# WKV recurrence on one core: loads moved to the SyncE queue, state rows to GpSimd, and a shorter state chain

## The chip, the core and the metric

The kernel runs on one core of a Trainium2 chip. The metric is the device time of one execution in microseconds (us). A core has a matrix engine (TensorE, PE in the profile), VectorE (DVE), ScalarE (ACT), GpSimd (POOL) and SyncE (SP). SP only issues transfers here; ACT and POOL can issue them too. All transfers are carried out by the core's 16 DMA engines. In the profile, transfers issued by POOL stand under the queue "software_dynamic", those issued by SP and ACT under "hardware_dynamic".

## The reference

For each of 16 batches and 256 channels the reference walks through 2048 time steps. Cut to what matters:

```
for t in range(seq_len):
    ww = u + k[t];  qq = max(pp, ww)
    e1, e2 = exp(pp - qq), exp(ww - qq)
    out[t] = (e1 * aa + e2 * v[t]) / (e1 * bb + e2 + 1e-08)
    ww = pp - w + k[t];  qq = max(ww, k[t])
    e1, e2 = exp(ww - qq), exp(k[t] - qq)
    aa, bb, pp = e1 * aa + e2 * v[t], e1 * bb + e2, qq
```

So the output is a weighted mean of all v so far, with weights exp(k) that decay by exp(-w) each step. `aa` and `bb` are numerator and denominator, `pp` is the running exponent that keeps them in range. Inputs k and v are 16 x 2048 x 256 float32 (33.5 MB each), and the output has the same size.

## The kernel before, in words

Time is cut into a head of 32 steps and 16 chunks ("steps" `c`, from 0 to 15) of 126 time steps. A chunk is worked on in four "pairs" `n` of four batches each; with two pairs for the head there are 66 pairs. A pair has time on the partitions and 4 batches x 256 channels along the free axis, so each of its three transfers (k in, v in, output) has about 512 KB.

The sum over time inside a chunk is a matrix product with triangular matrices. What comes from before the chunk, the state (the aa and bb above with their scale), is put into two extra rows (126 and 127) of the operand tiles `ez`. The state passes from chunk to chunk by a chain of small instructions on tiles of 128 partitions.

The main loop (L533) has one iteration per pair and works as a software pipeline. In iteration n:

- `load(n + 3)` starts the loads of `kr` and `vr`, each of which has four buffers (`AHEAD + 1`);
- ACT does `exps(n)` (L277), PE `sums(n - 1)` (L323), DVE rounds the next k, `round_k(n + 1)` (L258, tile `km`), and casts the next v, `cast_v(n + 1)` (L285, tile `vb`); DVE multiplies by v (L293);
- the output of a pair comes ten iterations after its exponentials (`LAG`): PE `den` and `num` (L457, L475), ACT the reciprocal as Ln and Exp (L465, L466), DVE `mult` (L483), and `store` (L499) for the pair of the iteration before.

Nothing is reordered by a planner: the helper `K` chains each instruction behind the last one of the same engine, so every engine and every issuing queue runs in the order in which Python emits it. That holds for the loads: those of pairs 0 to 3 are issued from SP (one of them from ACT), those of all later pairs from POOL (L121), where they stand in one line with the stores.

The state work of chunk c is spread by the table `later` (L503 to L516) over the iterations after the last pair of the chunk, s: the sums are copied and turned in s + 1 (`copy_sums`, `turn_sums`, `split_sums`). In s + 2 come the logs (`state_logs`, L352), the offsets S and exponents ex (`state_offsets`, L364 to L368), their exponentials g (`state_weights`, L375), and then the chain itself (`state_chain`, L387 to L392), which advances the state by two half chunks: tile `AB` holds numerator and denominator at both half-chunk starts. In s + 3 come the weights under which the state is injected (`inject_min` L402 and L404, `inject_weights` L409), the product `carries` (L417), the turn on PE (L424), the copy to `row` (L429) and four small transfers of 8 KB from SP (L433) that write `row` into rows 126 and 127 of `ez`. The tiles `ez` with these rows are first needed by `den` in iteration s + 7.

Of the kernel before, what the change touches and what calls it, by code (L numbers as in the profile page):

```python
# [22 lines left out]
def kernel(  # L23
# [11 lines left out]
    def K(ins):  # L35

        block, e, new = nc.cur_bb.bb, ins.ins.engine, []
        for i in reversed(block.instructions):
            if i.engine == e:
                new.append(i)  # L40
                if i.name == pinned.get(e):
                    break
        for a, b in zip(new[1:], new):
            tc.add_manual_dep(b, a.name, mybir.DependencyInfo(
                mybir.DependencyClass.NoSync, mybir.DependencyReason.DATA), reason="order")
        pinned[e] = new[0].name
        return ins
# [5 lines left out]
    TC = 2 * HS  # L53
    T0 = T % TC
    NST = T // TC
# [6 lines left out]
    RS = 2.0 ** -43  # L62
    LNRS = 43 * 0.6931471805599453
    CAP = 68.0

    consts = ctx.enter_context(tc.tile_pool(name="consts", bufs=1))
    kpool = ctx.enter_context(tc.tile_pool(name="kpool", bufs=AHEAD + 1))
# [33 lines left out]
    def load(n):  # L101
        kr = kpool.tile([128, 4, Dm], F32, tag="kr", name="kr")
        vr = vpool.tile([128, 4, Dm], F32, tag="vr", name="vr")
        kr_of[n], vr_of[n] = kr, vr
        c, p = pairs[n]
        if is_head(n):
            if p == 1:
                K(POOL.memset(kr[64:96, 0:2, :], 0.0))
                K(POOL.memset(vr[64:96, 0:2, :], 0.0))
            for t, x in ((kr, k), (vr, v)):  # L110
                for g in range(NG):
                    b = 6 * g + 4 * p
                    e = min(b + 2 * tiles_of(n), B)
                    if b < e:
                        K(SP.dma_start(out=t[g * GB:(g + 1) * GB, 0:e - b, :],
                                        in_=x[b:e, 0:T0, :].rearrange("n t d -> t n d")))
        else:
            t0 = T0 + c * TC
            r = min(128, T - t0)
            for t, x, eng in ((kr, k, SP), (vr, v, SP if n else SC)):  # L120
                K((eng if n <= AHEAD else POOL).dma_start(  # L121
                    out=t[0:r, :, :], in_=x[4 * p:4 * p + 4, t0:t0 + r, :].rearrange("n t d -> t n d")))


# [34 lines left out]
    K(POOL.memset(I1, 0.0))  # L159
    select(I1, NE, 1.0, 0, -1, 128, 1)  # L160
    K(POOL.memset(cc[:, 4:5], 0.5))
    select(cc[:, 4:5], GE, 0.0, -HS, 1, 1, 0)
    select(cc[:, 4:5], GE, 0.0, TC - 1, -1, 1, 0)

# [139 lines left out]
    def group_of(c, j):  # L304
        return 2 * j if c == 0 else 1 + 2 * c + j
# [37 lines left out]
    def split_sums(c):  # L343
# [2 lines left out]
        K(DVE.tensor_copy(t.rearrange("p r (b k) -> p (r b) k", k=4), tt))  # L346
        st[c, "t"] = t

    def state_logs(c):
        lf = tiny.tile([128, 2, 32], F32, tag="lf", name="lf")  # L350
        H = 1 if c < 0 else 2
        K(SC.activation(lf[:, 0:H], st[c, "t"][:, 4:4 + H], ACT.Ln))  # L352
        st[c, "lf"] = lf

    def state_offsets(c):

        lf = st.pop((c, "lf"))
        S = small.tile([128, 3, 32], F32, tag="S", name="S")
        ex = tiny.tile([128, 4, 32], F32, tag="ex", name="ex")
        if c < 0:  # L360
            K(DVE.tensor_copy(S[:, 2, :], lf[:, 0, :]))
            K(DVE.scalar_tensor_tensor(ex[:, 2, :], S[:, 2, :], 0.0, lf[:, 0, :], ALU.max, ALU.subtract))
        else:
            K(DVE.tensor_copy(S[:, 0, :], st.pop((c - 1, "S"))[:, 2, :]))  # L364
            for h in range(2):
                K(DVE.scalar_tensor_tensor(S[:, h + 1, :], S[:, h, :], 0.0, lf[:, h, :], ALU.max, ALU.add))
            K(DVE.tensor_scalar(ex[:, 0:2, :], S[:, 1:3, :], -1.0, 0.0, ALU.mult, ALU.max))
            K(DVE.scalar_tensor_tensor(ex[:, 2:4, :], S[:, 1:3, :], 0.0, lf, ALU.max, ALU.subtract))  # L368
        st[c, "S"] = S
        st[c, "ex"] = ex  # L370

    def state_weights(c):
        g = tiny.tile([128, 4, 32], F32, tag="g", name="g")
        sl = slice(2, 3) if c < 0 else slice(0, 4)
        K(SC.activation(g[:, sl, :], st.pop((c, "ex"))[:, sl, :], ACT.Exp, scale=-2.0))  # L375
        st[c, "g"] = g

    def state_chain(c):

        g, t = st.pop((c, "g")), st.pop((c, "t"))[:, 0:4].rearrange("p (q h) x -> p q h x", q=2)  # L380
        nxt = small.tile([128, 2, 2, 32], F32, tag="AB", name="AB")
        if c < 0:
            K(DVE.tensor_mul(nxt[:, :, 0, :], t[:, :, 0, :], g[:, 2:3, :].broadcast_to([128, 2, 32])))
        else:
            cur = AB[c]
            tb = tiny.tile([128, 2, 2, 32], F32, tag="tb", name="tb")
            K(DVE.tensor_mul(tb, t, g[:, 2:4, :].unsqueeze(1).broadcast_to([128, 2, 2, 32])))  # L387
            for h in range(2):
                dst = cur[:, :, 1, :] if h == 0 else nxt[:, :, 0, :]
                da = tiny.tile([128, 2, 32], F32, tag=f"da{h}", name=f"da{h}")  # L390
                K(DVE.tensor_mul(da, cur[:, :, h, :], g[:, h:h + 1, :].broadcast_to([128, 2, 32])))
                K(DVE.tensor_add(dst, da, tb[:, :, h, :]))  # L392
        AB[c + 1] = nxt

    def inject_logs(c):
        y = tiny.tile([128, 2, 32], F32, tag="y", name="y")
        K(SC.activation(y, AB[c][:, 0], ACT.Ln, scale=RS))
        st[c, "y"] = y

    def inject_min(c):  # L400
        m = tiny.tile([128, 2, 32], F32, tag="m", name="m")
        K(DVE.tensor_scalar(m, st.pop((c, "y")), -0.5, 0.5 * (CAP - LNRS), ALU.mult, ALU.add))  # L402
        m2 = tiny.tile([128, 2, 32], F32, tag="m2", name="m2")
        K(DVE.scalar_tensor_tensor(m2, st[c, "S"][:, 0:2, :], 0.0, m, ALU.max, ALU.min))  # L404
        st[c, "m"] = m2

    def inject_weights(c):
        f = tiny.tile([128, 2, 32], F32, tag="phi", name="phi")
        K(SC.activation(f, st.pop((c, "m")), ACT.Exp, scale=2.0))  # L409
        st[c, "phi"] = f  # L410

    def carries(c):

        ab = tiny.tile([128, 2, 2, 2, 16], BF16, tag="ab16", name="ab16")
        cur, f = AB.pop(c), st.pop((c, "phi"))
        for h in range(2):
            K(DVE.tensor_mul(ab[:, h].rearrange("p j q x -> p q j x"),  # L417
                             cur[:, :, h, :].rearrange("p q (j x) -> p q j x", j=2),
                             f[:, h, :].rearrange("p (j x) -> p j x", j=2).unsqueeze(1).broadcast_to([128, 2, 2, 16])))
        st[c, "ab"] = ab  # L420

    def turn_carries(c):
        d = bank("den", [128, 2, D])[:, 0]
        K(PE.matmul(d[:, 0:128], st.pop((c, "ab")).rearrange("p h j q x -> p (h j q x)"), Id, start=True, stop=True))  # L424
        st[c, "d"] = d

    def inject(c):
        row = small.tile([128, 128], BF16, tag="row", name="row")
        K(DVE.tensor_copy(row, st.pop((c, "d"))[:, 0:128]))  # L429
        for j in range(2):  # L430
            for h in range(2):
                p = 64 * h + 32 * j
                K(SP.dma_start(out=EZ[group_of(c, j)][TC + h:TC + h + 1, 0:2, :, :].rearrange(  # L433
                                   "o q i (x c) -> o (q i x) c", c=128),
                               in_=row[p:p + 32, :]))

# [67 lines left out]
    for c in range(-1, NST):  # L504
        s = last_of[c]
        work = [(s + 1, "sums", copy_sums), (s + 1, "last", turn_sums)]
        if c < 0:
            work += [(s + 2, "sums", split_sums), (s + 2, "act", state_logs), (s + 2, "last", state_offsets),
                     (s + 3, "exp", state_weights), (s + 3, "pool", state_chain)]
# [93 lines left out]
```

## Time and profile before

| | |
|---|---|
| median of 13 runs | 366.59 us (364.08 to 371.74) |
| the profiled execution: its own time | 366.59 us |
| its span, first to last instruction | 364.9 us |
| busy in the span: PE, DVE, ACT, POOL | 291.1, 295.4, 279.4, 168.7 us |
| moved by the DMA engines | 102.59 MB, 281 GB/s over the span |
| of it on the queue that POOL feeds | 98.53 MB |
| mean of one load issue on POOL (kr, vr) | 797 ns, 774 ns |
| mean of one store issue on POOL | 1000 ns |
| median from issue to landing, loads of 512 KB from POOL (kr, vr) | 8.0 us, 8.6 us |

The profiled execution took exactly the median, and 1.69 us of it lie outside the span. "Busy" adds up the time in which an engine had at least one instruction in work. The "chain that ended last" goes back from the last instruction, at each step to whatever released it. A DMA on that chain is time in which the work waited for data that had been asked for but had not landed.

### The profile page before, as it was taken

Reading aid. Unit: us, or ns where it says so; the run is one execution under the profiler, and the core shown is the slowest. Engines: PE = TensorE matmul, PEld = TensorE weight load, DVE = VectorE, ACT = ScalarE, POOL = GpSimd, SP = SyncE. Lnnn points to the kernel's source line nnn. Section 1 sums busy time; section 2 is a strip of 40 time slices with the busy share of each in tenths; the row PEclk is TensorE's granted clock in tenths of the full one; section 3 lists DMA queues with packets and bytes.
Section 4 is the critical chain, followed back from the end, with each engine's and each line's share of the span. In section 5 each row is a group of like instructions: output and inputs, shape, how many; then the busy total and the mean of one; then the engine's idle time right before and its main releaser. Section 6 shows DMA issues by size and latency. Waiting matters only on the chain.

```text
span 364.9 us, 4088 instructions
## 1 busy us (share of the span) xinstructions
PE 291.1 (80%) x1200; PEld 138.6 (38%) x1200; DVE 295.4 (81%) x636; ACT 279.4 (77%) x286; POOL 168.7 (46%) x224
## 2 busy tenths in 40 slices
PE   0568698788789797979898879979697879789780
PEld 0324344344334352434444434534343444333330
DVE  2667879879797998979998979898897989696651
ACT  2464669488788886977988878988797878787891
POOL 5433317725546363626465554636353736321331
PEclk9997989899999998989999998999999999999997
DMA  7998826896989899998999998999999899955575
GB/s 216 236 322 282 256 89 203 269 335 220 335 288 334 317 303 337 295 345 282 340 319 333 313 348 288 331 329 310 338 283 368 260 348 249 304 176 173 173 228 170
DMA packets 34982, 102.59 MB, mean 281 GB/s; under 512 B 7712, under 2 KB 10912, under 8 KB 34960
## 3 DMA queue, kind: packets, MB, share of 16 engines
q0 software_dynamic: 28432, 98.53, 82.3%
q1 hardware_dynamic: 5840, 3.15, 3.5%
q10 hardware_dynamic: 688, 0.66, 0.7%
q8 instruction: 9, 0.15, 0.2%
q14 instruction: 13, 0.11, 0.1%
HBM read 68.22 MB, written 33.55 MB: 279 GB/s over the span
## 4 chain that ended last, share of the span: by engine, by line
DMA 32%; DVE 27%; PE 25%; ACT 9%; issue 4%; POOL 1%; ACTq 0%; POOLq 0%; DVEq 0%
DMA kr<-in_k_dram 23%; DMA vr<-in_v_dram 9%; DVE rd L483 8%; PE X L266 7%; PE tot L323 6%; PE num L475 6%; DVE km L258 5%; DVE ez L293 4%; PE den L457 4%; ACT ez L277 3%; ACT rd L465 2%; DVE vb L285 2%; ACT rd L466 2%; PE den L339 2%; DVE AB L392 2%
## 5 line engine op out<-in xcount | busy, mean ns | idle before, releaser
L277 ACT ACTIVATE ez<-X 128x2048 bf16<-128x2048 f32 x66 | 122.2, 1852 | 18.3 <-PE X L266 18.3
L499 POOL DMA_DIRECT2D out_dram<-rd x64 | 64.0, 1000 | 154.2 <-DVE vb L285 52.2
L483 DVE TENSOR_TENSOR rd<-num,rd 126x512 f32<-126x512 f32 (+1 forms) x131 | 88.9, 685 | 11.0 <-ACT rd L466 8.4
L293 DVE TENSOR_TENSOR ez<-ez,vb 126x2048 bf16<-126x2048 bf16 (+1 forms) x66 | 79.9, 1211 | 7.1 <-ACT ez L277 6.2
L465 ACT ACTIVATE rd<-den 126x1024 f32<-126x1024 f32 (+1 forms) x66 | 66.6, 1010 | 19.7 <-PE den L457 18.7
L475 PE MATMUL num<-ez,LfN 128*128 128x512 bf16 x128 | 49.8, 389 | 34.9 <-DVE rd L483 34.3
L466 ACT ACTIVATE rd<-rd 126x1024 f32<-126x1024 f32 (+1 forms) x66 | 69.5, 1052 | 2.1
L266 PE MATMUL X<-km,NLE 128*128 128x512 f32 x128 | 54.3, 507 | 16.9 <-DVE km L258 13.5
L258 DVE CAST km<-kr 126x1024 fp32r<-126x1024 f32 x64 | 46.4, 725 | 25.1 <-DMA kr<-in_k_dram 20.2
L121 POOL DMA_DIRECT2D vr<-in_v_dram x62 | 48.0, 774 | 20.0 <-DVE vb L285 10.9
L323 PE MATMUL tot<-ez,OHV 126*48 126x512 bf16 x128 | 51.3, 401 | 7.1 <-DVE ez L293 7.0
L121 POOL DMA_DIRECT2D kr<-in_k_dram x62 | 49.4, 797 | 7.4 <-DVE km L258 5.0
L323 PE MATMUL tot<-ez,OHE 128*48 128x512 bf16 x128 | 52.6, 411 | 0.0
L475 PE MATMUL num<-ez,IdN 126*128 126x512 bf16 (+1 forms) x131 | 50.8, 388 | 0.0
L285 DVE CAST vb<-vr 126x1024 bf16<-126x1024 f32 (+1 forms) x66 | 44.9, 680 | 3.5 <-DMA vr<-in_v_dram 3.5
L266 PE MATMUL X<-km,NLZ 128*128 128x512 f32 x128 | 42.0, 411 | 0.0
L457 PE MATMUL den<-ez,Id 126*128 126x512 bf16 (+1 forms) x131 | 39.6, 382 | 0.0
L457 PE MATMUL den<-ez,Lf 128*128 128x512 bf16 x128 | 38.4, 380 | 0.0
L266 PEld LDWEIGHTS X<-km,NLE 128*128 128x128 f32 x128 | 25.0, 202 | 30.3 <-DVE km L258 9.8
L475 PEld LDWEIGHTS <-IdN 126*128 126x128 bf16 (+1 forms) x131 | 12.8, 98 | 53.4 <-issue 51.8
L266 PEld LDWEIGHTS X<-km,NLZ 128*128 128x128 f32 x128 | 25.4, 199 | 6.1
L323 PEld LDWEIGHTS <-OHE 128*48 128x48 bf16 x128 | 13.4, 104 | 32.6 <-issue 25.6
(96 smaller groups left out, 211.7 us busy)
## 6 DMA issues: line engine op xcount, KB each, us to landing
out_dram<-rd POOLq DMA_DIRECT2D x64, 504.0 KB, 6.8
kr<-in_k_dram POOLq DMA_DIRECT2D x58, 512.0 KB, 8.0
vr<-in_v_dram POOLq DMA_DIRECT2D x58, 512.0 KB, 8.6
kr<-in_k_dram POOLq DMA_DIRECT2D x4, 504.0 KB, 9.3
vr<-in_v_dram POOLq DMA_DIRECT2D x4, 504.0 KB, 10.3
kr<-in_k_dram SPq DMA_DIRECT2D x2, 512.0 KB, 4.7
ez<-row SPq DMA_DIRECT2D x64, 8.0 KB, 6.0
vr<-in_v_dram SPq DMA_DIRECT2D x1, 512.0 KB, 8.5
```

Source lines behind the costliest of these rows:

```text
L121: K((eng if n <= AHEAD else POOL).dma_start(out=t[0:r, :, :], in_=x[4 * p:4 * p + 4, t0:t0 + r, :].rearrange("n t d -> t n d")))
L258: K(DVE.tensor_copy(KM[n][0:r, 0:i, :], kr_of.pop(n)[0:r, 0:i, :]))
L266: K(PE.matmul(X[:, q, i, :], m[0:kr, :], km[0:kr, i, :], start=True, stop=True))
L277: K(SC.activation(ez_of(n)[:, 0:4:2], X_of.pop(n)[:, :, 0:i, :], ACT.Exp))
L293: K(DVE.tensor_mul(ez[0:r, 1:4:2], ez[0:r, 0:4:2], vb[0:r, 0:i, :].unsqueeze(1).broadcast_to([r, 2, i, D])))
L323: K(PE.matmul(TOT[c], m[0:r, :], ez_of(n)[0:r, q, i, :], start=n == first_of[c] and i == 0 and q == 0, stop=n == last_of[c] and i == tiles ...
L457: K(PE.matmul(d[:, i, :], m[0:r, :], ez_of(n)[0:r, q, i, :], start=q == 0, stop=q == 2, skip_group_check=True))
L465: K(SC.activation(rd[0:r, 0:i, :], DEN.pop(n)[0:r, 0:i, :], ACT.Ln, scale=RS))
L466: K(SC.activation(rd[0:r, 0:i, :], rd[0:r, 0:i, :], ACT.Exp, scale=-1.0))
L475: K(PE.matmul(d, m[0:r, :], ez_of(n)[0:r, q, i, :], start=q == 1, stop=q == 3, skip_group_check=True))
L483: K(DVE.tensor_mul(RD[n][0:r, i, :], NUM.pop((n, i))[0:r, :], RD[n][0:r, i, :]))
L499: K(POOL.dma_start(out=out[4 * p:4 * p + 4, t0:t0 + TC, :].rearrange("n t d -> t n d"), in_=o[0:TC, :, :]))
```

## The change

There are two parts.

The first part moves transfers between queues. All loads of k and v are now issued from SP (the very first v load stays on ACT), the four transfers of `row` per chunk go from SP to POOL, and the stores stay on POOL.

The second part rewrites the state chain. The running offset S lives in one persistent tile, so it is no longer copied at each chunk. The exponents are no longer formed on DVE with a maximum: S is clamped once (`near`), ACT takes exp(-2x) of it (`w`) and exp(2x) of it (`g`), and the "at most 1" is folded into the multiplies as `ALU.min`. The two state half steps are split: the first stays in s + 2, the second goes to s + 4 (s + 3 for chunk 0). The weights of injection come from one exponential with a bias, then one DVE instruction, and `carries` is one multiply instead of two.

```diff
-                K((eng if n <= AHEAD else POOL).dma_start(
+                K(eng.dma_start(
...
     def state_offsets(c):
-
         lf = st.pop((c, "lf"))
-        S = small.tile([128, 3, 32], F32, tag="S", name="S")
-        ex = tiny.tile([128, 4, 32], F32, tag="ex", name="ex")
...
-            K(DVE.tensor_copy(S[:, 0, :], st.pop((c - 1, "S"))[:, 2, :]))
-            for h in range(2):
-                K(DVE.scalar_tensor_tensor(S[:, h + 1, :], S[:, h, :], 0.0, lf[:, h, :], ALU.max, ALU.add))
-            K(DVE.tensor_scalar(ex[:, 0:2, :], S[:, 1:3, :], -1.0, 0.0, ALU.mult, ALU.max))
-            K(DVE.scalar_tensor_tensor(ex[:, 2:4, :], S[:, 1:3, :], 0.0, lf, ALU.max, ALU.subtract))
...
+        for h in range(2):
+            i = 2 * c + h
+            K(DVE.scalar_tensor_tensor(S[:, i + 1], S[:, i], 0.0, lf[:, h], ALU.max, ALU.add))
+        near = tiny.tile([128, 3, 32], F32, tag="near", name="near")
+        K(DVE.tensor_scalar(near, S[:, 2 * c:2 * c + 3], NEAR, -NEAR, ALU.min, ALU.max))
+        st[c, "near"] = near
+
+    def state_weights(c):
+        g = small.tile([128, 3, 32], F32, tag="g", name="g")
...
+            w = tiny.tile([128, 2, 32], F32, tag="w", name="w")
+            near = st.pop((c, "near"))
+            K(SC.activation(w, near[:, 0:2], ACT.Exp, scale=-2.0))
+            K(SC.activation(g, near, ACT.Exp, scale=2.0))
+            st[c, "w"] = w
...
-            K(DVE.tensor_mul(tb, t, g[:, 2:4, :].unsqueeze(1).broadcast_to([128, 2, 2, 32])))
-            for h in range(2):
-                dst = cur[:, :, 1, :] if h == 0 else nxt[:, :, 0, :]
-                da = tiny.tile([128, 2, 32], F32, tag=f"da{h}", name=f"da{h}")
-                K(DVE.tensor_mul(da, cur[:, :, h, :], g[:, h:h + 1, :].broadcast_to([128, 2, 32])))
-                K(DVE.tensor_add(dst, da, tb[:, :, h, :]))
-        AB[c + 1] = nxt
...
+    def state_step(c, h):
+        if h == 0:
+            t = st.pop((c, "t"))[:, 0:4].rearrange("p (q h) x -> p q h x", q=2)
+            tb = small.tile([128, 2, 2, 32], F32, tag="tb", name="tb")
+            K(DVE.scalar_tensor_tensor(tb, by_two(st.pop((c, "w"))), 1.0, t, ALU.min, ALU.mult))
+            st[c, "tb"] = tb
+        cur = AB[c]
+        if h == 1:
+            AB[c + 1] = small.tile([128, 2, 2, 32], F32, tag="AB", name="AB")
+        da = tiny.tile([128, 2, 32], F32, tag=f"da{h}", name=f"da{h}")
+        K(DVE.tensor_add(da, cur[:, :, h], st[c, "tb"][:, :, h]))
+        K(DVE.scalar_tensor_tensor(cur[:, :, 1] if h == 0 else AB[c + 1][:, :, 0], by_two(st[c, "g"][:, h + 1]), 1.0,
+                                   da, ALU.min, ALU.mult))
...
-    def inject_min(c):
-        m = tiny.tile([128, 2, 32], F32, tag="m", name="m")
-        K(DVE.tensor_scalar(m, st.pop((c, "y")), -0.5, 0.5 * (CAP - LNRS), ALU.mult, ALU.add))
-        m2 = tiny.tile([128, 2, 32], F32, tag="m2", name="m2")
-        K(DVE.scalar_tensor_tensor(m2, st[c, "S"][:, 0:2, :], 0.0, m, ALU.max, ALU.min))
-        st[c, "m"] = m2
...
-        K(SC.activation(f, st.pop((c, "m")), ACT.Exp, scale=2.0))
+        K(SC.activation(f, st.pop((c, "y")), ACT.Exp, scale=-1.0, bias=cc[:, 5:6]))
...
-        for h in range(2):
-            K(DVE.tensor_mul(ab[:, h].rearrange("p j q x -> p q j x"),
...
+        K(DVE.scalar_tensor_tensor(f2, st[c, "g"][:, 0:2], 1.0, f, ALU.max, ALU.min))
+        K(DVE.tensor_mul(ab, AB[c].rearrange("p q h (j x) -> p (h j) q x", j=2),
+                         f2.rearrange("p h (j x) -> p (h j) x", j=2).unsqueeze(2).broadcast_to([128, 4, 2, 16])))
...
-                K(SP.dma_start(out=EZ[group_of(c, j)][TC + h:TC + h + 1, 0:2, :, :].rearrange(
+                K(POOL.dma_start(out=EZ[group_of(c, j)][TC + h:TC + h + 1, 0:2, :, :].rearrange(
...
-                     (s + 2, "sums", state_offsets), (s + 2, "sums", state_weights), (s + 2, "pool", state_chain),
-                     (s + 2, "act", inject_logs), (s + 3, "first", inject_min), (s + 3, "exp", inject_weights),
+                     (s + 2, "sums", state_offsets), (s + 2, "sums", state_weights), (s + 2, "pool", first),
+                     (s + 2, "act", inject_logs), (s + 3, "exp", inject_weights),
...
+            if c + 1 < NST:
+                work.append((s + 4 if c else s + 3, "pool", second))
```

More of the change, by code (lines that the diff above doesn't have):

```diff
@@ L64 @@
     CAP = 68.0
+    NEAR = 44.0
     consts = ctx.enter_context(tc.tile_pool(name="consts", bufs=1))
@@ L161 @@
     K(POOL.memset(cc[:, 4:5], 0.5))
+    K(POOL.memset(cc[:, 5:6], CAP - LNRS))
     select(cc[:, 4:5], GE, 0.0, -HS, 1, 1, 0)
@@ L347, in split_sums @@
         st[c, "t"] = t
+    S = consts.tile([128, 2 * NST + 1, 32], F32, tag="S", name="S")
     def state_logs(c):
+        if c < 0:
+            K(SC.activation(S[:, 0], st[c, "t"][:, 4], ACT.Ln))
+            return
         lf = tiny.tile([128, 2, 32], F32, tag="lf", name="lf")
-        H = 1 if c < 0 else 2
-        K(SC.activation(lf[:, 0:H], st[c, "t"][:, 4:4 + H], ACT.Ln))
+        K(SC.activation(lf, st[c, "t"][:, 4:6], ACT.Ln))
         st[c, "lf"] = lf
@@ L360, in state_offsets @@
         if c < 0:
-            K(DVE.tensor_copy(S[:, 2, :], lf[:, 0, :]))
-            K(DVE.scalar_tensor_tensor(ex[:, 2, :], S[:, 2, :], 0.0, lf[:, 0, :], ALU.max, ALU.subtract))
-        else:
-            K(DVE.tensor_copy(S[:, 0, :], st.pop((c - 1, "S"))[:, 2, :]))
-            for h in range(2):
-                K(DVE.scalar_tensor_tensor(S[:, h + 1, :], S[:, h, :], 0.0, lf[:, h, :], ALU.max, ALU.add))
-            K(DVE.tensor_scalar(ex[:, 0:2, :], S[:, 1:3, :], -1.0, 0.0, ALU.mult, ALU.max))
-            K(DVE.scalar_tensor_tensor(ex[:, 2:4, :], S[:, 1:3, :], 0.0, lf, ALU.max, ALU.subtract))
@@ L369, in state_offsets @@
[L369 to L375, printed above, removed]
-        st[c, "g"] = g
[L378 to L386, printed above, removed]
-            K(DVE.tensor_mul(tb, t, g[:, 2:4, :].unsqueeze(1).broadcast_to([128, 2, 2, 32])))
-            for h in range(2):
-                dst = cur[:, :, 1, :] if h == 0 else nxt[:, :, 0, :]
-                da = tiny.tile([128, 2, 32], F32, tag=f"da{h}", name=f"da{h}")
-                K(DVE.tensor_mul(da, cur[:, :, h, :], g[:, h:h + 1, :].broadcast_to([128, 2, 32])))
-                K(DVE.tensor_add(dst, da, tb[:, :, h, :]))
-        AB[c + 1] = nxt
+            K(SC.activation(g[:, 0], S[:, 0], ACT.Exp, scale=2.0))
+        else:
+            w = tiny.tile([128, 2, 32], F32, tag="w", name="w")
[3 more added lines that the diff above has]
+            st[c, "w"] = w
@@ new lines, in state_weights, with by_two, state_start @@
+        st[c, "g"] = g
+    def by_two(x):
+        n = list(x.shape)
+        return x.unsqueeze(1).broadcast_to([n[0], 2] + n[1:])
+    def state_start(c):
+        AB[0] = small.tile([128, 2, 2, 32], F32, tag="AB", name="AB")
+        t = st.pop((c, "t"))[:, 0:4].rearrange("p (q h) x -> p q h x", q=2)
+        K(DVE.scalar_tensor_tensor(AB[0][:, :, 0], by_two(st.pop((c, "g"))[:, 0]), 1.0, t[:, :, 0],
+                                   ALU.min, ALU.mult))
+    def state_step(c, h):
+        if h == 0:
+            t = st.pop((c, "t"))[:, 0:4].rearrange("p (q h) x -> p q h x", q=2)
+            tb = small.tile([128, 2, 2, 32], F32, tag="tb", name="tb")
[8 more added lines that the diff above has]
+                                   da, ALU.min, ALU.mult))
@@ L398, in inject_logs @@
         st[c, "y"] = y
-    def inject_min(c):
-        m = tiny.tile([128, 2, 32], F32, tag="m", name="m")
-        K(DVE.tensor_scalar(m, st.pop((c, "y")), -0.5, 0.5 * (CAP - LNRS), ALU.mult, ALU.add))
-        m2 = tiny.tile([128, 2, 32], F32, tag="m2", name="m2")
-        K(DVE.scalar_tensor_tensor(m2, st[c, "S"][:, 0:2, :], 0.0, m, ALU.max, ALU.min))
-        st[c, "m"] = m2
     def inject_weights(c):
         f = tiny.tile([128, 2, 32], F32, tag="phi", name="phi")
-        K(SC.activation(f, st.pop((c, "m")), ACT.Exp, scale=2.0))
+        K(SC.activation(f, st.pop((c, "y")), ACT.Exp, scale=-1.0, bias=cc[:, 5:6]))
         st[c, "phi"] = f
     def carries(c):
-        ab = tiny.tile([128, 2, 2, 2, 16], BF16, tag="ab16", name="ab16")
-        cur, f = AB.pop(c), st.pop((c, "phi"))
-        for h in range(2):
-            K(DVE.tensor_mul(ab[:, h].rearrange("p j q x -> p q j x"),
-                             cur[:, :, h, :].rearrange("p q (j x) -> p q j x", j=2),
-                             f[:, h, :].rearrange("p (j x) -> p j x", j=2).unsqueeze(1).broadcast_to([128, 2, 2, 16])))
+        ab = tiny.tile([128, 4, 2, 16], BF16, tag="ab16", name="ab16")
+        f, f2 = st.pop((c, "phi")), tiny.tile([128, 2, 32], F32, tag="phi2", name="phi2")
+        K(DVE.scalar_tensor_tensor(f2, st[c, "g"][:, 0:2], 1.0, f, ALU.max, ALU.min))
+        K(DVE.tensor_mul(ab, AB[c].rearrange("p q h (j x) -> p (h j) q x", j=2),
+                         f2.rearrange("p h (j x) -> p (h j) x", j=2).unsqueeze(2).broadcast_to([128, 4, 2, 16])))
         st[c, "ab"] = ab
@@ L423, in turn_carries @@
         d = bank("den", [128, 2, D])[:, 0]
-        K(PE.matmul(d[:, 0:128], st.pop((c, "ab")).rearrange("p h j q x -> p (h j q x)"), Id, start=True, stop=True))
+        K(PE.matmul(d[:, 0:128], st.pop((c, "ab")).rearrange("p m q x -> p (m q x)"), Id, start=True, stop=True))
         st[c, "d"] = d
@@ L506 @@
         work = [(s + 1, "sums", copy_sums), (s + 1, "last", turn_sums)]
+        first, second = lambda c: state_step(c, 0), lambda c: state_step(c, 1)
         if c < 0:
-            work += [(s + 2, "sums", split_sums), (s + 2, "act", state_logs), (s + 2, "last", state_offsets),
-                     (s + 3, "exp", state_weights), (s + 3, "pool", state_chain)]
+            work += [(s + 2, "sums", split_sums), (s + 2, "act", state_logs),
+                     (s + 3, "exp", state_weights), (s + 3, "pool", state_start)]
         else:
             work += [(s + 1, "last", split_sums), (s + 2, "first" if c else "exp", state_logs),
-                     (s + 2, "sums", state_offsets), (s + 2, "sums", state_weights), (s + 2, "pool", state_chain),
-                     (s + 2, "act", inject_logs), (s + 3, "first", inject_min), (s + 3, "exp", inject_weights),
+                     (s + 2, "sums", state_offsets), (s + 2, "sums", state_weights), (s + 2, "pool", first),
+                     (s + 2, "act", inject_logs), (s + 3, "exp", inject_weights),
                      (s + 3, "pool", carries), (s + 3, "last", turn_carries), (s + 3, "last", inject)]
+            if c + 1 < NST:
+                work.append((s + 4 if c else s + 3, "pool", second))
         for slot, where, f in work:
```

## The prediction

> **What bounds the kernel now.** I read the page first. All three compute engines are busy about 80% of the span, which decides nothing. The chain that ended last has one large foreign body:
>
> ```profile
> DMA 32%; DVE 27%; PE 25%; ACT 9%; issue 4%; POOL 1%; ACTq 0%; POOLq 0%; DVEq 0%
> q0 software_dynamic: 28432, 98.53, 82.3%
> ```
>
> A third of the chain is waiting for transfers, and nearly all bytes go through the one queue that POOL feeds. Next, the chain in order of time: one late load of k or v (7.6 to 9.9 us from issue to landing) per chunk from 70 us on. The first late k load starts at 70.11 and the one twelve chunks later at 303.73, so a chunk lasts 233.62 / 12 = 19.47 us. One of them in the chain:
>
> ```profile
> 207.51 0.41 DVE rd L483
> 207.91 8.58 DMA kr<-in_k_dram
> 216.49 0.02 issue
> 216.52 0.94 DVE km L258
> ```
>
> The waits of DVE from 60 to 312 us, the 13 chunks with loads and stores together, give its direct price, and POOL's instructions show why the load is late:
>
> ```profile
> DVE km L258 <- DMA kr<-in_k_dram: 19.2, 19, 1.9
> ```
>
> ```profile
> 202.62 1.29 POOL L499 DMA_DIRECT2D out_dram<-rd  x1 [4.92 <-issue]
> 203.91 0.77 POOL L121 DMA_DIRECT2D kr<-in_k_dram  x1
> 204.67 0.75 POOL L121 DMA_DIRECT2D vr<-in_v_dram  x1
> 206.80 1.12 POOL L499 DMA_DIRECT2D out_dram<-rd  x1 [1.38 <-ACT rd L466]
> 207.91 0.77 POOL L121 DMA_DIRECT2D kr<-in_k_dram  x1
> ```
>
> DVE stood still 19.2 / 13 = 1.48 us per chunk for k. The load at 207.91 starts the moment the store ahead of it is issued. Its buffer had been free since 197.4 (DVE started the cast four pairs back at 196.71 and took 0.69), so it was asked for 10.5 us later than it could have been.
>
> Is the DMA itself full? The stretches of time say "nearly, but not at one speed" (busy us and count of PE, PEld, DVE, ACT, POOL, then PE clock, DMA share, GB/s):
>
> ```profile
> 217.00:223.00 6.00, 3.97 (x12) 1.41 (x11) 5.69 (x18) 4.50 (x7) 0.52 (x1) 0.77 0.99 377
> 223.00:228.00 5.00, 5.00 (x22) 2.38 (x21) 4.67 (x10) 3.46 (x4) 3.21 (x4) 0.94 0.78 219
> 226.00:227.00 1.00, 1.00 (x6) 0.34 (x4) 1.00 (x3) 1.00 (x2) 0.00 (x0) 1.00 0.92 143
> ```
>
> While POOL writes no descriptors and the queue has a backlog of loads and a store, the engines move 377 GB/s. While POOL is issuing, 219, and once 143 at a share of 0.92. The mean over 200 to 300 us is 319 GB/s. What a chunk needs is 8 loads of 524,288 B and 4 stores of 516,096 B, 6.26 MB, or 321 GB/s at 19.47 us. So the DMA is the limit only at its slow speed. The first line also shows the PE clock at 0.77 after PE had idled through the stall.
>
> **What the Trainium skill says.** "SBUF — State Buffer", section "Who interferes with whom": transfers issued by GpSimd need GpSimd to write their descriptors through ports that it shares with VectorE; a VectorE copy or cast in a two-port mode shuts it out, and transfers issued by SP or ACT don't suffer. The trace agrees in outline: slow stretches coincide with POOL issuing, the issue of a store takes 807 to 1298 ns, and DVE's casts (L258 and L285, about 0.68 us for 1024 elements, which is over one element per cycle of 0.96 GHz) run twice per pair. It does not isolate the lock. "DMA: Bandwidth & Descriptors", section "Issuing engines are not separate DMA queues": all issuers share the same 16 engines, so a move to another queue brings no bandwidth as such. Its section "Queues, rings and completion order": each engine takes turns between queues, packet by packet. POOL's packets here average 98.53 MB / 28432 = 3.5 KB, while SP's loads use about 1 KB (337 packets for 0.34 MB from 5 to 6 us). So where both wait, stores may get some 3.5 bytes to a load's one. No run here shows large loads from SP beside stores.
>
> **The change, part by part.**
>
> *Loads to SP.* 62 + 62 loads leave POOL: 124 issues of about 0.79 us, 97 us of POOL's 168.7. POOL isn't the bound, so this alone is worth nothing. What counts is that a load no longer stands behind a store that waits for DVE's multiply. On SP it waits only for its own buffer, and the late one above could start at 197.5 instead of 207.9. At the same 8.6 us it would land at 206, with 9 us in hand before DVE needs it at 215. Nothing else runs on SP: before, it waited there 224.6 us from 60 to 312 for `row`. Can loads from SP be fast? Only the start shows it: from 8 to 9 us, with both hardware queues and nothing else,
>
> ```profile
> DMA packets 389, 0.39 MB, mean 385 GB/s; under 512 B 13, under 2 KB 389, under 8 KB 389
> q1 hardware_dynamic: 232, 0.22, 65.0%
> q10 hardware_dynamic: 157, 0.16, 45.8%
> ```
>
> and 337 GB/s from 5 to 6 us with 99% on SP's queue. So 1 KB packets are not slow in themselves. Gain, bounded: nothing (the DMA stays at 321 GB/s) to 19.2 us (no wait). I take 80%, 15.4 us, because without the stall the DMA has to carry 350 GB/s (below), and some waits will remain.
>
> *Rows to POOL.* 64 issues. The nearest row is the head's stores from POOL, 0.56 us each, so 4 x 0.56 = 2.2 us per chunk on POOL, which loses 6.3 us of load issues. Behind them stand only stores. Before, a row landed in 6.0 us; its reader is four iterations (some 18 us) later, and the reuse of `rd` buffers also leaves about four iterations. I put 0. At the end iterations take about 2.1 us: the last row is copied at 339.9, the four issues would follow the store at 340.6 and end near 343.7, landing by 347; `den` wants it around 348. If that cover is gone, 1 to 3 us, once.
>
> *State chain on DVE*, by the starts in the timeline, so with the waits between small dependent instructions. Removed per chunk: the copy of S 0.27 (217.38 to 217.65) and two exponents against one clamp, 0.24 - 0.12 = 0.12; `m` and `m2` 0.37 (241.61 to 241.98). Chain: five instructions took 1.12 (218.94 to 220.06); now 0.67 in s + 2 and 0.41 in s + 4, a saving of 0.04. `carries` 0.27 becomes about 0.45, since the multiply waits for the weights: a loss of 0.18. Sum 0.27 + 0.12 + 0.37 + 0.04 - 0.18 = 0.62 us per chunk, 9.9 us in 16. Bounds: 0 (ACT or DMA sets the pace) to 9.9; in s + 2 PE and ACT wait for this very work (ACT `g` for `ex` 11.7 us, PE `num` for `rd` 28.7 us from 60 to 312), so much of it is on the path. I take half, 5 us.
>
> *ACT* gets one exponential more per chunk, 0.22 us by the start distance of `g` to the next (237.68 to 237.90), 3.5 us in all. ACT is busy 16.6 of 20 us, so it lies in idle time: 0; with that gone, 3.5.
>
> *Casts.* L258 takes 725 ns in the mean and 673 at best; if that is GpSimd holding the ports, 64 x 0.05 = 3 us of DVE come back. I count it inside the 80%. The start is left at 0: SP reaches pair 4's loads near 15 us instead of POOL's 10 to 14, and DVE needs them at 24.9.
>
> Sum: -15.4 - 5 = -20.4 us. Against the span of 364.9 that gives 344.5; with the 1.7 us outside it, 346.2. The profiled execution equals the median, 366.59, so I predict **346 us**. A cross-check: 20.4 less over 13 chunks and a little at the edges means about 17.9 us per chunk, hence 6.26 / 17.9 = 350 GB/s, 93% of the 377 that it reached with a full queue.
>
> **The rivals.**
>
> *The DMA remains the bound* (chance 0.18). For it: its share is 0.92 to 0.98 in every 20 us from 100 to 300, and stores still come from POOL. Against it: two thirds of the bytes no longer depend on POOL. If the mixed rate stops at 330 GB/s, a chunk takes 19.0 us, 0.5 x 13 = 6 us are won, and the state chain's gain hides behind the DMA: 360 us.
>
> *Mixing the queues slows the DMA* (0.07, slower). Stores take turns in big packets and loads in small ones; from 16 to 17 us, with both kinds in flight, the trace moved only 195 GB/s, though with narrow head loads of 32 partitions. It decides from 321 GB/s downwards: at 300 a chunk takes 20.9 us, 13 x 1.4 = +18: 385 us.
>
> *More than the named waits goes* (0.13). Stalls vanish wholly (19.2), the state saving counts in full (9.9), and PE keeps its clock and DVE its ports (3): 334 us. Against it: it needs 6.26 / 17.2 = 364 GB/s.
>
> *The queue change does nothing and ACT's extra work cancels the chain's gain* (0.02): 366 us. The remaining 0.60 is the forecast.
>
> **From cases to numbers.** A difference of 0.5% (1.8 us) is about what a measurement of this kernel can tell. Faster: 0.60 + 0.13 + 0.17 of the DMA rival = 0.90; same 0.03; slower 0.07. The range runs from the fast case to the DMA-bound one, 334 to 360.
>
> **What would show it.** Right: k's wait on DVE under 5 us in the stage, chunks of about 18 us, GB/s about 345 to 355, SP loads issued some 10 us before POOL's place, POOL busy near 110 us. Wrong: the DMA share at 1.0 with 320 to 330 GB/s and k still waited for (rival one); load landings beyond 15 us with stores landing fast (rival two); PE waiting for `row` transfers at the end.

## The result, and the profile after

The changed kernel takes 341.79 us in the median of 11 runs (340.11 to 343.20), the kernel before 366.48 us in the median of 48. That is 24.7 us less. The ratio is 0.938 with a 95% interval of 0.9352 to 0.9409, so 6.2% faster. The ratio, like the medians of the experiments further on, counts only fast runs (a run more than 1.5% above the fastest of its kernel is a slow one), and so it comes out a little smaller than the two medians make it. The profiled execution has a span of 342.6 us, against 364.9.

The page of the changed kernel, first the chain that ended last by engine, then the two large DMA queues (packets, MB, share of 16 engines):

```profile
PE 45%; DVE 26%; ACT 13%; DMA 7%; issue 6%; POOL 1%; ACTq 0%; POOLq 0%; DVEq 0%
q1 hardware_dynamic: 68160, 67.58, 62.8%
q0 software_dynamic: 12496, 34.11, 28.6%
```

DMA fell from 32% to 7% of the chain. Two thirds of the bytes now go through SP's queue, in packets of 67.58 MB / 68160 = 1.0 KB.

The waits of DVE from 60 to 300 us of the changed kernel (us in total, times, longest), all that were listed:

```profile
DVE tsum L348 <- PE den L341: 8.5, 14, 4.3
DVE tb L399 <- ACT w L379: 5.2, 14, 0.4
DVE ez L295 <- ACT ez L279: 0.5, 1, 0.5
```

The wait for k, 19.2 us before (17.9 in this window), is gone. A new one has come: `tb` waits about 0.37 us per chunk for ACT's `w`. The wait of `tsum` has grown as well; before, in the same window, it was

```profile
DVE tsum L346 <- PE den L339: 1.8, 5, 0.6
```

Of the 8.5 us now, 4.3 are one wait at chunk 1 (more on it below). The rest is about 0.3 us per chunk.

The stretch from 100 to 200 us, the changed kernel first and the kernel before second (busy us and count of PE, PEld, DVE, ACT, POOL; then PE clock, DMA share, GB/s):

```profile
100.00:200.00 100.00, 94.58 (x408) 45.51 (x407) 95.15 (x181) 93.68 (x101) 33.72 (x47) 1.00 1.05 357
```

```profile
100.00:200.00 100.00, 87.76 (x369) 42.04 (x369) 89.91 (x186) 84.52 (x88) 51.65 (x60) 0.97 0.94 317
```

PE, DVE and ACT are all within 7% of full now, while the DMA carries 357 instead of 317 GB/s, and PE keeps its full clock.

Where the 22.3 us of span went can be read from the starts of one instruction per chunk, the copy of the sums (`tsum`). It stands at 58.90 us for chunk 1 and 333.5 for chunk 15 before, at 62.70 and 308.5 after. So the fourteen chunks between them are 28.8 us shorter, the stretch up to chunk 1 is 3.8 us longer, and the end 2.7 us longer. One chunk in the middle, counted from chunk 2 to chunk 13, takes (274.54 - 79.09) / 11 = 17.77 us, against (294.69 - 77.13) / 11 = 19.78 before.

### The profile page after: what moved, and what is told of

It reads as the page before. It is cut to its first block, busy times and chain, and to the rows that moved or that the text cites. A ratio compares the mean times of both kernels' runs of the same rounds, so it can differ in the third digit from the quotient of the medians.

```text
span 342.6 us, 4126 instructions
## 1 busy us (share of the span) xinstructions
PE 291.7 (85%) x1200; PEld 139.7 (41%) x1200; DVE 282.6 (82%) x568; ACT 279.1 (81%) x302; POOL 100.8 (29%) x165
## 3 DMA queue, kind: packets, MB, share of 16 engines
q1 hardware_dynamic: 68160, 67.58, 62.8%
q0 software_dynamic: 12496, 34.11, 28.6%
## 4 chain that ended last, share of the span: by engine, by line
PE 45%; DVE 26%; ACT 13%; DMA 7%; issue 6%; POOL 1%; ACTq 0%; POOLq 0%; DVEq 0%
PE X L268 14%; PE num L482 11%; PE tot L325 10%; ACT ez L279 7%; DVE rd L490 6%; DVE ez L295 6%; PE den L464 5%; DVE km L260 5%; PE den L341 4%; DMA ez<-row 4%; DMA vr<-in_v_dram 3%; DVE vb L287 3%; ACT rd L473 2%; ACT rd L472 1%; DVE tsum L348 1%
## 5 line engine op out<-in xcount | busy, mean ns | idle before, releaser
L506 POOL DMA_DIRECT2D out_dram<-rd x64 | 59.3, 926 | 186.7 <-DVE rd L490 65.6
L472 ACT ACTIVATE rd<-den 126x1024 f32<-126x1024 f32 (+1 forms) x66 | 66.8, 1012 | 13.1 <-PE den L464 12.6
L268 PE MATMUL X<-km,NLE 128*128 128x512 f32 x128 | 54.3, 507 | 15.7 <-DVE km L260 13.2
L325 PE MATMUL tot<-ez,OHV 126*48 126x512 bf16 x128 | 50.6, 395 | 9.6 <-DVE ez L295 9.6
L325 PE MATMUL tot<-ez,OHE 128*48 128x512 bf16 x128 | 51.6, 403 | 0.0
L260 DVE CAST km<-kr 126x1024 fp32r<-126x1024 f32 x64 | 45.0, 704 | 4.8 <-ACT km L194 4.8
L440 POOL DMA_DIRECT2D ez<-row x64 | 33.1, 523 | 45.6 <-DVE km L260 45.6
L482 PEld LDWEIGHTS <-LfN 128*128 128x128 bf16 x128 | 12.4, 97 | 31.7 <-issue 23.2
```

The source lines that it names most:

```text
L260: K(DVE.tensor_copy(KM[n][0:r, 0:i, :], kr_of.pop(n)[0:r, 0:i, :]))
L268: K(PE.matmul(X[:, q, i, :], m[0:kr, :], km[0:kr, i, :], start=True, stop=True))
L325: K(PE.matmul(TOT[c], m[0:r, :], ez_of(n)[0:r, q, i, :], start=n == first_of[c] and i == 0 and q == 0, stop=n == last_of[c] and i == tiles ...
L472: K(SC.activation(rd[0:r, 0:i, :], DEN.pop(n)[0:r, 0:i, :], ACT.Ln, scale=RS))
L482: K(PE.matmul(d, m[0:r, :], ez_of(n)[0:r, q, i, :], start=q == 1, stop=q == 3, skip_group_check=True))
L506: K(POOL.dma_start(out=out[4 * p:4 * p + 4, t0:t0 + TC, :].rearrange("n t d -> t n d"), in_=o[0:TC, :, :]))
```

## The experiments

Every table value "chunk" is worked out like the two numbers just given, from the starts of `tsum`. "Lead" is worked out too: the time from the start of the issue of a k load to the start of the cast that needs it, median between 90 and 290 us. Medians are in us; "before" is the kernel before in the same group of runs (in the first two rows, in all groups together).

| run | median | before | ratio, 95% interval | chunk | lead | wait for k, 60 to 300 us | L258 cast, mean ns |
|---|---|---|---|---|---|---|---|
| kernel before | 366.48 | | | 19.78 | 9.5 | 17.9 | 725 |
| changed kernel | 341.79 | 366.48 | 0.938 (0.9352 to 0.9409) | 17.77 | 17.1 | 0 | 704 |
| queues only | 353.15 | 365.26 | 0.966 (0.9584 to 0.9743) | 18.63 | 17.7 | 0 | 791 |
| chain only | 352.20 | 365.26 | 0.964 (0.9549 to 0.974) | 18.75 | 8.8 | 13.9 | 728 |
| loads earlier, from POOL | 351.02 | 365.26 | 0.962 (0.955 to 0.9693) | 18.49 | 13.5 | 0 | 745 |
| stores to SP, loads on POOL | 344.91 | 365.26 | 0.943 (0.9348 to 0.9502) | 18.27 | 17.3 | 0 | 685 |
| all on SP, old order | 350.30 | 366.39 | 0.958 (0.9507 to 0.9651) | 18.36 | 8.0 | 1.8 | 686 |

### The two halves of the change

The queues alone, on the kernel before:

```diff
-                K((eng if n <= AHEAD else POOL).dma_start(
+                K(eng.dma_start(
...
-                K(SP.dma_start(out=EZ[group_of(c, j)][TC + h:TC + h + 1, 0:2, :, :].rearrange(
+                K(POOL.dma_start(out=EZ[group_of(c, j)][TC + h:TC + h + 1, 0:2, :, :].rearrange(
```

> The kernel before with only the queue part of the change (loads on SP, rows on POOL, old state chain). If the queues are the main cause, as forecast, k's wait on DVE is nearly gone and the time is 347 to 353 us (15 to 19 us less than before). If the shorter chain were the main cause, under 8 us are gained: above 358 us.

The chain alone is the changed kernel with these two lines put back:

```diff
-                K(eng.dma_start(
+                K((eng if n <= AHEAD else POOL).dma_start(
...
-                K(POOL.dma_start(out=EZ[group_of(c, j)][TC + h:TC + h + 1, 0:2, :, :].rearrange(
+                K(SP.dma_start(out=EZ[group_of(c, j)][TC + h:TC + h + 1, 0:2, :, :].rearrange(
```

> The changed kernel with the old queues (loads from POOL, rows from SP), so the new state chain alone. Forecast: 5 us less than before, 361 us. If the late loads set the pace of the stage, DVE's gain turns into a longer wait for k (over 25 us instead of 19.2 us from 60 to 312 us) and the time stays within 2 us of before. If the chain alone were worth its full 10 us: 356 us.

The queues gave 12.1 us; their 353.15 us lie at the edge of what was expected. The chain gave 13.1 us, over twice the forecast, though its interval is wide (0.9549 to 0.974 is 9.5 to 16.5 us). The two sum to 25.2 us, about what the whole change gave, so neither hides the other. The chunks say the same more closely: 1.15 us and 1.03 us less by each alone, 2.01 us less by both. Two waits of DVE with the chain alone:

```profile
DVE km L260 <- DMA kr<-in_k_dram: 13.9, 21, 1.4
DVE tb L399 <- ACT w L379: 0.6, 2, 0.4
```

The wait for k fell too, from 17.9 to 13.9 us, although not one transfer had moved to another queue. And the DMA went from 317 to 339 GB/s between 100 and 200 us, so the old rate was not the most that this queue could carry. In the code a load is issued behind a store, and that store waits for DVE's multiply; a faster DVE therefore asks for its data earlier. That this is what took 4.0 us off the wait is argued; no run isolates it. "The chain's gain becomes a longer wait" is refuted.

### Late issue or descriptors

Loads still from POOL, one iteration earlier:

```diff
-        if 0 < n and n + AHEAD < NP:
-            load(n + AHEAD)
+        if n + AHEAD + 1 < NP:
+            load(n + AHEAD + 1)
```

> The kernel before, with each load emitted one iteration earlier (load(n + 4) instead of load(n + 3) in iteration n, still four buffers, still from POOL). Theory 'late issue': what hurt was that a load stood behind a store; with 4 to 5 us more in hand the wait for k falls below 8 us and the time is 348 to 356 us. Theory 'descriptors': the DMA is slow because POOL has to write the descriptors of the loads; then earlier issue only makes the queue longer, the rate stays at about 320 GB/s and the time at 362 to 368 us.

The queues the other way round (both store statements, the head's too):

```diff
-            K(POOL.dma_start(out=out[4 * p:4 * p + 4, t0:t0 + TC, :].rearrange("n t d -> t n d"),
+            K(SP.dma_start(out=out[4 * p:4 * p + 4, t0:t0 + TC, :].rearrange("n t d -> t n d"),
```

> The kernel before with the roles of the queues the other way round: loads stay on POOL, stores go to SP beside the rows. No load stands behind a store any more, but POOL still writes the descriptors of all loads. Theory 'late issue': as good as the queue part of the change, 347 to 354 us. Theory 'descriptors': two thirds of the bytes still come from POOL, the rate stays near 320 to 330 GB/s and the time is above 358 us.

Everything on SP in the old order (the edit above together with the loads on SP, rows as before):

> The kernel before with loads, stores and rows all on SP, in the old order: a load again stands behind the store of the iteration before, but GpSimd writes no descriptor at all. Theory 'late issue': no better than before by more than the few us of faster casts and of the end, 358 to 366 us, with k still waited for. Theory 'descriptors': as good as the queue part of the change, 345 to 354 us.

The first two speak for late issue: with loads from POOL and 4 us more lead, or without a store ahead of them, the wait for k is zero. The third contradicts it as the only cause. There a load again stands behind a store, its lead is even shorter than before (8.0 us in the median, 5.0 at the least, against 9.5 and 6.5), and still the wait nearly vanishes:

```profile
DVE km L258 <- DMA kr<-in_k_dram: 1.8, 3, 0.9
```

Issued from SP, the same load, asked for as late, is there in time: of the ten loads with less than 6 us of lead between 90 and 290 us, one was waited for, while before loads with leads of up to 9.3 us were. Either remedy is enough by itself, more lead or faster landing; how much of each the change itself needed is not shown. That the speed comes from POOL no longer having to write descriptors fits, but no run isolates it from the other differences between the queues.

What separates the three versions with the old chain and no wait for k is the cast L258. The page rows, first with only the queues changed (stores and rows on POOL), then with the stores on SP:

```profile
L258 DVE CAST km<-kr 126x1024 fp32r<-126x1024 f32 x64 | 50.7, 791 | 4.8 <-ACT km L192 4.8
```

```profile
L258 DVE CAST km<-kr 126x1024 fp32r<-126x1024 f32 x64 | 43.9, 685 | 4.9 <-ACT km L192 4.9
```

106 ns times 64 casts are 6.8 us of DVE. The chunks follow the casts: against the stores on SP, a cast is 106 ns longer with only the queues changed and 60 ns longer with the loads earlier, which is 0.42 and 0.24 us for the four casts of a chunk; the chunks are 0.36 and 0.22 us longer. In the timeline with only the queues changed, POOL's and DVE's rows at two places:

```profile
190.13 0.83 POOL L499 DMA_DIRECT2D out_dram<-rd  x1 [1.85 <-ACT rd L466]
```

```profile
190.47 0.98 DVE L258 CAST km<-kr 126x1024 fp32r<-126x1024 f32 x1
```

```profile
200.94 1.15 POOL L499 DMA_DIRECT2D out_dram<-rd  x1 [3.68 <-issue]
```

```profile
201.08 0.68 DVE L258 CAST km<-kr 126x1024 fp32r<-126x1024 f32 x1
```

At the first place the cast begins 0.34 us after a store's issue on POOL and takes 0.98 instead of 0.69 us. This happens about twice per chunk (again at 196.46 and 196.75). At the second place the cast begins after 0.14 us and keeps its length, and the issue takes 1.15 instead of 0.83 us. All 64 casts of this trace fit: the 23 that began 0.29 to 0.38 us after the start of a store's issue took 0.95 to 1.01 us; the 15 that began 0.09 to 0.26 us after it, and the 26 others, took 0.67 to 0.69. The Trainium skill, "SBUF — State Buffer", section "Who interferes with whom", says of the shared ports that issue order decides which of the two is blocked. The trace agrees that one of the two pays, but the order of the starts does not tell which: POOL began first at both places.

In the code a store waits for DVE's multiply, and casts come right behind that, so the two keep meeting. With the loads on POOL and the stores on SP they meet less: the longest L258 took 766 ns. The casts account for about half of the step from the queue part as made (12.1 us) to the reverse arrangement (20.4 us): from chunk 1 to chunk 13 the traces differ by 3.9 us. Another 3.1 us lie at the end, from the last `tsum` to the end of the span (32.2 against 29.0 us). The profiled execution of the reverse arrangement took 349.90 us; in it ACT waited 2.7 us for a store near the end, and the chunk there, outside the range of the table, took 21.97 us.

### Combining the reverse arrangement with the chain

This is the chain alone with the stores moved to SP as above.

> The new state chain with the queues the other way round: loads from POOL, stores and rows from SP. If the two gains add as they do in the change (chain about 10 us, stores on SP about 20 us), 334 to 338 us, better than the changed kernel. If the chunk is at the limit of DVE and ACT in any case, only the end gets shorter, by about 3 us: 338 to 340 us.

It gave 341.78 us (ratio 0.934, 0.9251 to 0.942), the time of the changed kernel, and so missed both of its expectations: the gains did not add. Its chunk is 17.76 us, the same as 17.77. All eight traces with the new chain and without the late loads have chunks of 17.76 to 17.78 us, whichever queue carries the loads and the stores, so the transfers no longer set this pace. What is left is the order of work on DVE, ACT and PE; which link of it holds the chunk is not shown. The casts of the changed kernel were already down to 704 ns: none of them begins between 0.14 and 0.52 us after a store's issue, and the longest takes 0.80 us. In the reverse arrangement with the new chain they take 715 ns, and in two places ACT waited for a store (in an execution of 344.42 us):

```profile
ACT rd L472 <- DMA out_dram<-rd: 4.0, 2, 3.0
```

### The rows of chunk 0

The changed kernel's waits of PE and of DVE from 45 to 66 us:

```profile
PE den L464 <- DMA ez<-row: 2.2, 1, 2.2
```

```profile
DVE tsum L348 <- PE den L341: 4.3, 1, 4.3
```

For chunk 0 the rows are written in iteration 8 and read in iteration 10, not four iterations later as for the other chunks. Two attempts:

```diff
-                K(POOL.dma_start(out=EZ[group_of(c, j)][TC + h:TC + h + 1, 0:2, :, :].rearrange(
+                K((POOL if c else SC).dma_start(out=EZ[group_of(c, j)][TC + h:TC + h + 1, 0:2, :, :].rearrange(
```

> The changed kernel with the row transfers of chunk 0 alone issued from ACT, a queue without a backlog. The trace after shows PE waiting 2.2 us and DVE 4.3 us around 58 to 62 us for these rows. If that wait is a cost of moving the rows beside the early loads, 2 to 4 us are gained: 338 to 340 us. If something else holds chunk 1 at this place, within 1 us of the changed kernel (341.8 us).

The second is the same edit with `SP` in place of `SC`; in its group the changed kernel was run once more.

> The changed kernel once more, as it is, so that the three runs beside it have it on the same chip: 341 to 345 us.

> The changed kernel with the rows of chunk 0 alone on SP, where they stand ahead of the loads of pair 12 and later. If the 2.2 us wait of PE for these rows comes from loads that were issued before them and share the 16 engines, holding those loads back behind the rows should take most of it away: PE's wait below 1 us and 2 to 3 us less than the changed kernel. If the rows are late because of the loads already under way (pair 11 and before), nothing is gained.

From ACT nothing was gained (344.01 us; ratio 0.941, 0.9349 to 0.9473): PE's wait for the rows is no longer listed, but ACT itself waited 2.1 us for them before an `ez`, and DVE waited 2.5 us for that `ez`. On SP, ahead of later loads, PE's wait is gone and the median is 339.12 against 342.00 us. The intervals of the two ratios, 0.936 (0.926 to 0.9456) and 0.942 (0.931 to 0.9533), overlap, and so do the six runs of each (338.18 to 341.00 and 338.99 to 343.97 us). The place of `tsum` of chunk 1 does not decide either, because it differs by 2 us between two executions of the changed kernel (62.70 and 60.74). Counted from `tsum` of chunk 0, chunk 1 comes 19.4, 18.8 and 17.9 us later in the three traces that have these rows on POOL beside the loads (the changed kernel, its repeat, and the version with late stores on SP below), and 15.7 and 17.1 us later in the two that have them on SP. So the gain is likely about 2 us. It speaks for traffic as what delays the rows, rather than the queue that they stand in. All transfers from 52 to 56 us of the changed kernel, and from 51 to 55 us with the rows of chunk 0 on SP:

```profile
DMA packets 1157, 1.09 MB, mean 272 GB/s; under 512 B 77, under 2 KB 1157, under 8 KB 1157
```

```profile
DMA packets 193, 0.03 MB, mean 9 GB/s; under 512 B 192, under 2 KB 193, under 8 KB 193
```

### The end, and the best versions

The last eight stores from SP:

```diff
-            K(POOL.dma_start(out=out[4 * p:4 * p + 4, t0:t0 + TC, :].rearrange("n t d -> t n d"),
+            K((SP if n >= NP - 8 else POOL).dma_start(out=out[4 * p:4 * p + 4, t0:t0 + TC, :].rearrange("n t d -> t n d"),
```

> The changed kernel with the last eight stores issued from SP instead of POOL. With stores from POOL 7 us pass from the start of the last issue to the end of the span, with stores from SP about 4 us. If the issuing queue makes this difference, 2.5 to 3.5 us are gained: 338.5 to 339.5 us. If the end is the landing of the data, nothing changes: 341.8 us.

It missed: 344.97 us (ratio 0.943, 0.9354 to 0.9502), no better than the changed kernel. From the last issue's start to the end of the span it is indeed about 4.6 us instead of 7.6 (335.02 to 342.6 in the changed kernel), but the waits of ACT at the end show what it cost:

```profile
ACT rd L472 <- DMA out_dram<-rd: 9.8, 2, 7.0
```

The `rd` buffer of a pair is used again five pairs later, and at the end an iteration takes only about 2 us. So a sixth `rd` buffer was added to two versions: to the rows of chunk 0 on SP with only the last two stores on SP, and to the new chain with loads on POOL, stores and rows on SP.

```diff
-    rpool = ctx.enter_context(tc.tile_pool(name="rpool", bufs=5))
+    rpool = ctx.enter_context(tc.tile_pool(name="rpool", bufs=6))
```

> As the last one, with six instead of five buffers for rd (so that no reciprocal waits for a store to land) and the last two stores issued from SP. The wait for stores at the end goes, and the end after the last issue shrinks from 7 to about 4 us: 3 us less than with the rows of chunk 0 on SP alone, 5 to 6 us less than the changed kernel.

> The new state chain with loads from POOL, stores and rows from SP, and six buffers for rd. In the version with five buffers ACT waited 4.0 us for stores in two places. With these gone, 337 to 339 us; if stores of 126 partitions from SP simply take too long to land, the waits remain: 341 to 343 us.

They took 335.37 us (ratio 0.926, 0.9143 to 0.9375) and 336.37 us (0.927, 0.9131 to 0.9408), beside 342.00 for the changed kernel in the same group. ACT no longer waits for a store in either. By the medians they beat the changed kernel by 6.6 and 5.6 us, and all runs that count in them (333.69 to 337.69 and 334.05 to 337.99 us) lie below its lowest (338.99). The intervals against the kernel before overlap with the changed kernel's in this group, so the size of the step is not settled. Both still have chunks of 17.8 us, so the gain must lie at the ends. The trace of the second shows it there: 28.7 us from the last `tsum` to the end of the span, against 32.3 in the repeat of the changed kernel. The trace of the first is of an execution of 341.14 us and does not show where it gains; in it the end after the last issue shrank less than expected, from 7.6 to about 5.8 us.

## Why the prediction was right, point by point

**The total: near, in part by luck.** The prediction had 20.4 us, from 15.4 for the queues and 5 for the chain. Alone, the parts gave 12.1 and 13.1 us. One was set too high and the other too low, so that their sum came nearer than the parts.

**What bounded the kernel: right, one link missing.** The late k loads did set the pace, and they are gone. The working took the DMA's rate as a limit in reserve, and it was not one: 357 GB/s flow now. One line was misread: from 226 to 227 us, at 143 GB/s, POOL issued nothing (0.00 (x0)), so POOL's issuing does not account for every slow stretch. The prediction's chunk of 19.47 us was also a little short, because the last of the late loads it counted from stood at another place in its chunk; 19.78 is measured.

**Loads to SP, -15.4 us: the sign and mechanism right, the size too large.** The run with the queues alone gave 12.1 us. Loads are asked for 17.1 us ahead of their cast instead of 9.5, and the whole wait of 19.2 us went, not 80%. Against it stand two costs put at nothing or with the wrong sign. The casts were to get back 3 us; with the queues alone they became slower (725 to 791 ns, 66 ns x 64 = 4.2 us more), because 23 of them now begin 0.29 to 0.38 us after the start of a store's issue. In the full change they are 704 ns, 1.3 us less. The second cost is the rows.

**Rows to POOL, 0: wrong at one place.** The cover named was "four iterations (some 18 us) later". For chunk 0 it is two, and its rows now travel beside early loads: PE waited 2.2 us for them (1.5 in the repeat). With these rows ahead of the loads the wait is gone and the median is 2.9 us lower, a size that the scatter leaves open. The feared wait at the other end, for the last chunk, did not appear: no wait of PE for rows is listed after 290 us.

**State chain, -5 us: mis-sized, it gave 13.1 us alone.** The range taken, 0 to 9.9 us, counted only the instructions removed from DVE. The failing step is "much of it is on the path; I take half". With the chain alone the gain was above the whole range, and k's wait, which this term left out, fell by 4.0 us as well; the full 9.9 and these 4.0 would make 13.9. Why k's wait fell is argued above, not shown. On top of the moved queues the chain brought the chunk from 18.63 to 17.77 us. Of these 0.86 us, 4 x 87 ns = 0.35 are the casts, which went from 791 to 704 ns; 0.51 are left, beside the 0.62 that the prediction had added up.

**ACT's extra exponential, 0: open.** In the changed kernel DVE waits for `w`, 0.37 us per chunk, 5.2 us from 60 to 300 us. The same chain with the old queues has the same exponentials and waits only 0.6 us there, so the extra one alone does not make the wait. Whether it is part of what holds the chunk at 17.77 us, no run shows.

**The rivals.** "The DMA remains the bound" is refuted: 339 GB/s with the old queues and the new chain, 357 with both. "Mixing the queues slows the DMA" is refuted for these loads and stores. "More than the named waits goes" came nearer than its chance of 0.13 suggested: the wait went whole and the chain was worth more than half. Against it stood the rows of chunk 0, the new waits for `w` and of `tsum`, and an end that is 2.7 us longer. Of that end, about two thirds differ from execution to execution (32.3 us from the last `tsum` in the repeat, 34.1 in the first profile, 31.4 before); the rest stays open.

**The signs named.** k's wait under 5 us: 0. Chunks of about 18 us: 17.77. 345 to 355 GB/s: 357. Loads some 10 us earlier: their lead grew by 7.6 us. POOL busy near 110 us: 100.8, since an issue of a row took 0.52 us and the stores got shorter (926 ns).

## What to carry to other kernels

In a queue that issues in order, a load behind a store whose data is computed late is asked for late as well, and a delay of computing can feed back into the next load. Here it cost 12 us or more until the loads had more lead or landed faster. Compare the lead of a load, from issue to the instruction that needs it, with its landing time, before one takes a busy DMA for a full one. When transfers are moved between queues, look at what the remaining issuer now collides with, and at the first and last trip of the pipeline, where the slack is not that of the steady state.

## What the runs showed of the hardware that was not expected

- Issuing stores from GpSimd can cost VectorE time: the cast of 126x1024 float32 takes 685 ns in the mean with the stores on SP, 791 ns with the queues alone changed and the stores on GpSimd. In that trace who pays goes with the distance of the two starts: a cast that begins 0.29 to 0.38 us after the issue takes 0.95 to 1.01 us, one that begins 0.09 to 0.26 us after it takes 0.68 to 0.69 us, and then the issue is longer (1.11 to 1.28 instead of 0.81 to 0.84 us).
- Loads in packets of 1 KB on SP's queue, beside GpSimd's queue with stores and rows (34.11 MB / 12496 = 2.7 KB per packet in the mean), reached 357 GB/s over 100 us. GpSimd's queue with loads and stores, in packets of 3.5 KB, had carried 317 to 341.
- Transfers of 8 KB can take as long to land as far larger ones: the rows took 6.0 us in the median from SP before (1.8 at the least) and 7.2 us from GpSimd in the changed kernel (2.9 at the least), the stores of 504 KB there 7.5 us.
- From the start of the last store's issue to the end of the span, 6.3 to 7.6 us pass when it comes from GpSimd (eight traces) and 4.2 to 4.6 us when all late stores come from SP (five traces). But in the middle of the end phase a store from SP kept ACT waiting 7.0 us for a buffer, so a faster finish is not a faster landing of each store. Why, no run shows.
